# A hybrid layer's experts: rows gathered as the pair before is turned, indices one pair sooner, place 6's pages loaded in front of a test

## The chip, the cores and the metric

The kernel runs on one core of a Trainium2 chip. The metric is the device time of one execution in microseconds (us), as the median of several runs. TensorE (PE) multiplies, VectorE (DVE) and ScalarE (ACT) work element by element, GpSimd (POOL) issues the indirect DMAs and SyncE (SP) issues the loads of weights.

## What is computed

One layer: a mixer of retention, mLSTM and dilated attention, a layer norm, then a mixture of 32 experts over 512 tokens of width 1024, and a last layer norm. Each token goes to its top 4 experts. The change lies in the mixture; this is its reference, cut to what matters:

```python
logits = (xt @ w_router + b_router).astype(jnp.float32)      # 512 x 32
top_val, top_idx = lax.top_k(logits, TOP_K)                  # 4 of 32
probs = jax.nn.softmax(top_val, axis=-1)
...                                # rows of one expert stand in blocks of 128
def block(acc, inp):
    e, tok, p = inp
    xb = xt[tok]                                             # gathered rows
    gate = jnp.minimum(xb @ w_gate[e] + b_gate[e], SWIGLU_LIMIT)
    up = jnp.clip(xb @ w_up[e] + b_up[e], -SWIGLU_LIMIT, SWIGLU_LIMIT)
    y = ((up + 1.0) * gate * jax.nn.sigmoid(SWIGLU_ALPHA * gate)) @ w_down[e] + b_down[e]
    return acc.at[tok].add(y * p[:, None]), None
```

w_gate, w_up and w_down of an expert are 1024 x 1024 in float32, 4 MB each, so 384 MB of weights pass through the core.

## The kernel before

**Places and pages.** Experts are ranked by their number of tokens and put on 32 places (`ranks`, `placed`). Place 0 and the odd places take up to 96 rows, the other even places up to 64 (`small`, `size`). A place has 12 pages of weights, 128 x 2048 floats (1 MB) each: four each of gate, up and down, by halves of the output (`nh`) and of the input (`kh`). SP loads a page into one of ten raw buffers (`raws`, `fetch`, `load`, L85). ACT rounds it to float32r (`split_to`, L89) and DVE takes the rest (L90), and PE multiplies high and low parts (L117, L957). One page in twelve is used whole and not split (`unsplit`, L966). `chunk_of` splits up to two pages ahead of the one that PE wants.

**Pairs.** After places 0 and 1 the loop runs over pairs (e, e + 1), e = 2, 4, ..., 28. In the step of e stand, in this order of writing: gate and up of the pair (`gate_up_of`), every second step the indices of the next four places (`indices`, `IB` = 4), the gathers of the next pair (`gather_of`), and the down products of the pair before (`down_and_add`). Between the two halves of these, the next pair's rows are turned (`turned_x`: PE transposes to `txT`, L896 for 96 rows, L909 for 64, then ACT and DVE split them).

**Rows.** `indices` makes one-hot tiles on DVE (L636), multiplies them on PE (L1022) and finishes on DVE (L644 to L648, into `gi` and `wi`). `gather_of` is an indirect DMA of POOL (L940) from `x1d` in HBM into `xgs[e % 2]`: one buffer for the small places and one for the others, so a gather can start once the place two before is turned. `scatter` (L945) adds results from `ygs[e % 2]` to `yb` in HBM; each scatter waits until the one before has landed.

**The test.** At e = `FB` = 6 the order is another one: the down products of places 4 and 5 follow those of 2 and 3 at once, and then `further_blocks` tests a count (`novi`, L1060, L1069) and runs a loop over blocks that did not fit. With these inputs the count is zero. Every engine takes the test as a branch. In `chunk_of` pages of place 6 are not taken up before e is 6, and in the queues none of them is loaded or split in front of the test; on SP 28 register loads for later pages (L851) stand there. Place 7 is turned only behind the test, and 8 and 9 at the end of that step.

**Order.** A scheduler builds the queues of the engines from the order of writing, the dependences and its own estimates; on each engine instructions then run in the order of its queue, so one that waits holds up those behind it.

Of the kernel before, what the change touches and what calls it, by code (L numbers as in the profile page):

```python
# [20 lines left out]
E = 32  # L21
# [20 lines left out]
def hybrid_layer(ctx: ExitStack, tc: tile.TileContext, A, out):  # L42
# [11 lines left out]
    rp = [cst.tile([128, PAGE], F32R, tag=f"r{i}", name=f"r{i}") for i in range(NR)]  # L54
# [17 lines left out]
    raws = [fp[0], fp[1]]  # L72
# [29 lines left out]
    whi, wlo = [rp[4], rp[5]], [rp[6], rp[7]]  # L102
# [726 lines left out]
    FB = 6  # L829
# [29 lines left out]
    def flush():  # L859
        while later:  # L860
            later.pop(0)()

    def chunk_of(e):

        def f(n, nh, kh):
            last = seq[n, e, nh, kh] + len(whi) - 1
            while todo and seq[todo[0]] <= last and todo[0][:2] != ("w_down", L) and (todo[0][1] != FB or e >= FB):
                k = todo.pop(0)
                if k not in loaded:
                    fetch(1)  # L870
                w = loaded.pop(k)
                ready[k] = (w, None) if unsplit(k) else w if isinstance(w, tuple) else split_whole(w)
            with ExitStack() as es:
                for i in last_split:
                    es.enter_context(tc.issue_after(i))
                flush()
            return ready.pop((n, e, nh, kh))
        return f
# [12 lines left out]
    def transposed(src, name, page, m=C, whole=None):  # L891
        hl_ = page[:, 0:16 * m].rearrange("p (w a b) -> p w a b", w=2, a=8)
        for i in range(2):
            p = ps(f"t{name}_{i}")
            for k in range(4):
                PE.transpose(p[:, m * k:m * k + m], src[0:m, blk(4 * i + k)], ident[0:m, 0:m])  # L896
            s = slice(4 * i, 4 * i + 4)
            split_to(hl_[:, 0, s, :], hl_[:, 1, s, :], v3(p, 4, 4 * m))
            if whole is not None and i == 0:
                SC.activation(whole, v3(p, 4, 4 * m), AF.Copy)  # L900
        return hl_[:, 0], hl_[:, 1], whole
# [114 lines left out]
    def indices(e0, n):  # L1016
        p = ps(f"ix{e0}")
        for e in range(e0, e0 + n):
            j = 5 * (e - e0)
            o = one_hot(e, f"oh{e}")  # L1020
            for tb in range(NT):
                PE.matmul(p[0:C, j:j + 5], o[:, tb], RH[:, tb, e, :], start=tb == 0, stop=tb == NT - 1)  # L1022
        index_finish(p, n, C, gi[:, e0:e0 + n], wi[:, e0:e0 + n], f"ixf{e0}")
# [4 lines left out]
    def gate_up_of(*es, between=None):  # L1028
        parts = []
        for e in es:  # L1030
            if small(e):
                f = folds[e // 2 % 2]
                PO.tensor_copy(f[0:64, 0:CS], selr[0:64, e:e + 1].bitcast(F32).to_broadcast([64, CS]))
            parts.append((str(e), chunk_of(e), f if small(e) else selr[:, e:e + 1], xT.pop(e), hgs[e % 2], size(e), small(e)))
        return gate_up(parts, between)
# [22 lines left out]
    def further_blocks():  # L1058

        nov = nc.values_load(novi[0:1, 0:1], min_val=0, max_val=NB - 1)  # L1060
        jcol = cst.tile([NB, 4], F32, name="jcol")
        erow = cst.tile([1, NB], I32, name="erow")
        jrow = cst.tile([128, NB], F32, name="jrow")
        qe = cst.tile([128, NT, 1], F32, name="qe")
        je = cst.tile([128, 1], F32, name="je")
        re = cst.tile([128, NT, 1, 5], BF, name="re")
        gio = cst.tile([128, 1], I32, name="gio")
        wio = cst.tile([128, 1], F32, name="wio")
        with tc.If(nov > 0):  # L1069

            c0, c1, sml, c3 = (cnt[0:NB, i, :] for i in range(4))
            V.tensor_scalar(c0, c1, num[0:NB, 1:2], None, op0=OP.is_le)
            V.tensor_reduce(jcol[:, 0:1], c0, axis=AX.X, op=OP.add)
            V.tensor_tensor(c3, c1, c0, op=OP.mult)
            V.tensor_reduce(jcol[:, 1:2], c3, axis=AX.X, op=OP.max)
            V.tensor_scalar(jcol[:, 0:1], jcol[:, 0:1], float(E - 1), None, op0=OP.min)
            V.scalar_tensor_tensor(c3, iota_e[0:NB], jcol[:, 0:1], sml, op0=OP.is_equal, op1=OP.mult, accum_out=jcol[:, 3:4])
            V.tensor_scalar(jcol[:, 2:3], num[0:NB, 1:2], jcol[:, 1:2], 1.0, op0=OP.subtract, op1=OP.add)
            V.tensor_scalar(jcol[:, 2:3], jcol[:, 2:3], 128.0, float(C - 128), op0=OP.mult, op1=OP.add)
            V.tensor_tensor(jcol[:, 2:3], jcol[:, 2:3], jcol[:, 3:4], op=OP.subtract)  # L1080
            p = ps("ove")
            PE.transpose(p[0:1, 0:NB], jcol[:, 0:1], ident[0:NB, 0:NB])
            V.tensor_copy(erow, p[0:1, 0:NB])
            p = ps("ovj")
            PE.matmul(p[:, 0:NB], jcol[:, 2:3].to_broadcast([NB, 128]), ident[0:NB, 0:NB], start=True, stop=True)
            V.tensor_copy(jrow, p[:, 0:NB])
            main_raws = list(raws)
            raws[:] = raws[-1:]
            with tc.For_i(0, nov) as b:
                ev = nc.values_load(erow[0:1, ds(b, 1)], engines=(nc.sync.engine, nc.vector.engine), min_val=0, max_val=E - 1)  # L1090
                xv = nc.values_load(srt["of"][0:1, ds(ev, 1)], engines=(nc.sync.engine,), min_val=0, max_val=E - 1)
                V.tensor_copy(qe, qs[:, :, ds(ev, 1)])
                V.tensor_copy(je, jrow[:, ds(b, 1)])
                V.tensor_copy(re, RH[:, :, ds(ev, 1), :])
                V.tensor_copy(selr[:, E:E + 1], selr[:, ds(ev, 1)].bitcast(F32))
                p = ps("ovx")
                for tb in range(NT):
                    o = sm.tile([128, NT, C], BF, tag="ohs", name=f"ovo{tb}").rearrange("p t c -> p (t c)")[:, 0:128]
                    V.tensor_scalar(o, iota_s, je, qe[:, tb, :], op0=OP.add, op1=OP.is_equal)
                    PE.matmul(p[:, 0:5], o, re[:, tb, 0, :], start=tb == 0, stop=tb == NT - 1)  # L1100
                index_finish(p, 1, 128, gio, wio, "ixov")
                xo = v3(fp[11], 2)[:, 1, :]
                V.memset(xo, 0.0)
                gather(xo, gio)
                xTo = transposed(xo, "xTo", rp[0], 128)

                def chunk(n, nh, kh):
                    flush()
                    return split_whole(load(A[n][ds(xv, 1), nh, kh].rearrange("e p k f -> p (e k) f"), 4))

                gate_up([("o", chunk, selr[:, E:E + 1], xTo, hgs[0], 128, False)])
                flush()
                ho = transposed(hgs[0], "hTo", rp[1], 128)
                down([("o", chunk, ho, ygs[0], wio, 128, False)])
                flush()
                scatter(ygs[0], gio)
            cleared_folds()
            raws[:] = main_raws

    IB = 4  # L1120

# [18 lines left out]
    def turned_x(e):  # L1140
        if small(e):
            xT[e] = transposed_small(xgs[0], f"xT{e}", rp[2][:, 0:HALF])
        else:
            xT[e] = transposed(xgs[e % 2], f"xT{e}", rp[0], whole=xw)

    def gather_of(e):
        gather(xgs[e % 2][0:size(e)], gi[0:size(e), e:e + 1])
# [18 lines left out]
    PO.memset(xgs[0], 0.0)  # L1166
    turned_x(1)
    gate_up_of(1, between=first_indices)
    flush()
    for i, t in ((2, whi), (3, wlo)):  # L1170
        t.insert(0, cst.tile([128, PAGE], F32R, tag=f"f{i}", name=f"s{i}"))
# [16 lines left out]
    for e in range(2, L - 1, 2):  # L1188
        if e == FB:
            down_and_add(*before)  # L1190
            flush()
            further_blocks()
            turned_x(FB + 1)
        gate_up_of(e, e + 1)
        if e % IB == 2:
            indices(e + 2, IB if e + 2 + IB <= E else E - e - 2)
        for f in (e + 2, e + 3):
            if f < L:
                gather_of(f)
        if e == FB - 2:  # L1200
            count_blocks()
        def turned_next():
            for f in (e + 2, e + 3):
                if f < L and f != FB + 1:
                    turned_x(f)

        if e != FB:
            down_and_add(*before, between=turned_next)
        before = (e, e + 1)
        if e == FB:  # L1210
            flush()
        for f in before:
            turned_h(f)
        if e == FB:
            turned_next()
# [8 lines left out]
            PE.matmul(p, ident[0:1, 0:1].to_broadcast([1, 128]), ln2[0:1, i, c], start=True, stop=True)  # L1224
            SC.activation(ln2[:, i, c], p, AF.Copy)
    gate_up_of(L - 1)
    gather_of(L)
    PO.memset(rows, 0.0)
    down_and_add(*before)
    flush()  # L1230
    turned_h(L - 1)
    turned_x(L)
    down_and_add(L - 1)
    flush()
    zt = [v3(t, 2) for t in extra[1:3]]
# [168 lines left out]
```

## Time and profile before

| what | value |
|---|---|
| median of 3 runs | 1858.97 us |
| lowest and highest | 1857.85 and 1859.48 us |
| profiled execution, its own time | 1858.14 us |
| its span, first to last instruction | 1856.0 us |
| mean granted TensorE clock | 0.966 |
| PE, DVE and ACT busy | 92%, 69%, 58% of the span |

The span is 2.1 us shorter than the execution's own time. The first gather of an expert's rows starts at 642.7 us and the last scatter at 1808.1 us. Times in rows of a timeline are counted from the start of the span. The clock in a row of windows is the granted share of full speed: 1.00 is 2.4 GHz, 0.50 is 1.2 GHz.

### The profile page before, as it was taken

What the parts mean: (1) busy time and instruction counts of PE and PEld (TensorE: products, weight loads), DVE (VectorE), ACT (ScalarE), POOL (GpSimd) and SP (SyncE); (2) the same over time, 40 slices, a digit from 0 to 9 for tenths busy, and PEclk for the clock granted to TensorE, in tenths of its full rate; (3) what the DMA queues carried; (4) which work ended last, traced back from release to release, by engine and by line L of the source; (5) the groups of instructions that cost most, each with busy time, mean ns of one, the idle gap of its engine ahead of it and who ended that gap; (6) DMA issues with size and microseconds to landing.
All of it is one profiled execution on the core that took longest, in us unless ns stands there. A gap on an engine that the chain in (4) does not pass through costs nothing. (4 is left out here: it accounts for less than half of the span.)

```text
span 1856.0 us, 21811 instructions
## 1 busy us (share of the span) xinstructions
PE 1706.1 (92%) x7566; PEld 1245.6 (67%) x7566; DVE 1275.5 (69%) x1342; ACT 1078.1 (58%) x1097; POOL 234.4 (13%) x133
## 2 busy tenths in 40 slices
PE   8999999999999899797989799899989989979886
PEld 6889877778888666564656566566656656656553
DVE  3444255654354888786778698788878868878776
ACT  4464325532232457575667587587677767867781
POOL 0000000000000410201110220220220220130114
PEclk9999999999999989898889999999989989989898
DMA  5212212153243469897989999989989989988795
GB/s 207 90 52 108 87 60 93 56 188 127 95 162 137 169 241 342 308 405 261 360 302 364 377 327 405 382 315 405 384 292 411 374 306 409 375 325 355 252 330 223
DMA packets 73808, 485.24 MB, mean 261 GB/s; under 512 B 9914, under 2 KB 10170, under 8 KB 18782
## 3 DMA queue, kind: packets, MB, share of 16 engines
q1 hardware_dynamic: 65742, 460.58, 64.2%
q0 software_dynamic: 7952, 23.22, 4.9%
q8 instruction: 61, 1.00, 0.2%
q14 instruction: 53, 0.43, 0.1%
HBM read 471.30 MB, written 16.91 MB: 263 GB/s over the span
## 5 line engine op out<-in xcount | busy, mean ns | idle before, releaser
L90 DVE TENSOR_TENSOR r<-f,r 128x2048 fp32r<-128x2048 f32 (+3 forms) x249 | 450.8, 1818 | 281.8 <-ACT r L89 272.7
L89 ACT ACTIVATE r<-f 128x2048 fp32r<-128x2048 f32 (+3 forms) x249 | 380.0, 1536 | 192.5 <-PE pg L117 35.1
L117 PE MATMUL gu<-r,r 128*96 128x512 f32 x924 | 233.4, 398 | 3.0 <-DVE r L90 2.3
L117 PEld LDWEIGHTS gu<-r,r 128*96 128x96 f32 x924 | 148.8, 163 | 68.9 <-DVE r L90 5.2
L957 PE MATMUL gu<-r,xh 128*128 128x512 f32 x632 | 183.3, 422 | 4.0 <-DVE r L90 3.6
L90 DVE TENSOR_TENSOR s<-f,s 128x2048 fp32r<-128x2048 f32 x68 | 155.4, 2286 | 23.0 <-ACT s L89 18.8
L117 PE MATMUL dn<-r,h 128*96 128x512 f32 x516 | 144.6, 415 | 27.5 <-ACT r L89 22.5
L90 DVE TENSOR_TENSOR r<-g,r 128x2048 fp32r<-128x2048 f32 x68 | 154.9, 2287 | 19.3 <-ACT r L89 19.1
L957 PEld LDWEIGHTS gu<-r,xh 128*128 128x128 f32 x632 | 120.4, 192 | 50.0 <-issue 15.8
L945 POOL DMA_INDIRECT yb<-f,gi x31 | 80.9, 2609 | 533.6 <-ACT f L1012 432.1
L89 ACT ACTIVATE r<-g 128x2048 fp32r<-128x2048 f32 x68 | 129.8, 1918 | 26.3 <-PE gu L117 13.6
L117 PE MATMUL pg<-x,r 128*128 128x512 f32 x576 | 138.5, 399 | 0.0
L89 ACT ACTIVATE s<-f 128x2048 fp32r<-128x2048 f32 x68 | 129.8, 1909 | 13.2 <-PE gu L117 4.2
L117 PEld LDWEIGHTS dn<-r,h 128*96 128x96 f32 x516 | 82.2, 169 | 74.0 <-ACT r L89 28.5
L117 PEld LDWEIGHTS pg<-x,r 128*128 128x128 f32 x576 | 107.9, 188 | 25.4 <-issue 0.2
L940 POOL DMA_INDIRECT f<-x1d,gi x31 | 82.5, 2660 | 251.7 <-DVE wi L648 102.6
L957 PE MATMUL dn<-r,xh 128*128 128x512 f32 x328 | 96.8, 419 | 4.7 <-DVE r L90 4.0
L957 PE MATMUL gu<-s,xh 128*128 128x512 f32 x328 | 94.7, 419 | 5.1 <-DVE s L90 3.6
L117 PE MATMUL gu<-s,r 128*96 128x512 f32 x372 | 93.3, 395 | 0.5 <-DVE s L90 0.5
L89 ACT ACTIVATE xh<-txT 128x256 fp32r<-128x256 f32 x30 | 11.3, 383 | 120.7 <-PE txT L909 120.5
L957 PEld LDWEIGHTS gu<-s,xh 128*128 128x128 f32 x328 | 61.9, 191 | 28.7 <-DVE s L90 6.8
L90 DVE TENSOR_TENSOR s<-g,s 128x2048 fp32r<-128x2048 f32 x32 | 73.2, 2287 | 7.7 <-ACT s L89 7.6
(387 smaller groups left out, 2683.5 us busy)
## 6 DMA issues: line engine op xcount, KB each, us to landing
f<-in_w_gate_dram SPq DMA_DIRECT2D x80, 1024.0 KB, 6.4
f<-in_w_up_dram SPq DMA_DIRECT2D x79, 1024.0 KB, 7.5
f<-in_w_down_dram SPq DMA_DIRECT2D x77, 1024.0 KB, 11.5
g<-in_w_down_dram SPq DMA_DIRECT2D x39, 1024.0 KB, 12.5
g<-in_w_up_dram SPq DMA_DIRECT2D x34, 1024.0 KB, 9.7
g<-in_w_gate_dram SPq DMA_DIRECT2D x32, 1024.0 KB, 6.8
l<-in_w_gate_dram SPq DMA_DIRECT2D x16, 1024.0 KB, 7.2
l<-in_w_up_dram SPq DMA_DIRECT2D x15, 1024.0 KB, 8.7
```

The source lines that it names most:

```text
L89: a = SC.activation(hi, src, AF.Copy)
L90: last_split[:] = [a.ins, V.tensor_tensor(lo, src, hi.bitcast(F32), op=OP.subtract).ins]
L117: PE.matmul(po, l(k), r(k), start=first and n == 0, stop=last and n == 3 * len(ks) - 1)
L940: nc.gpsimd.indirect_dma_start(out=dst, out_offset=None, in_=src, in_offset=bass.IndirectOffsetOnAxis(ap=idx, axis=0), bounds_check=S - 1, ...
L945: nc.gpsimd.indirect_dma_start(out=yb, out_offset=bass.IndirectOffsetOnAxis(ap=idx, axis=0), in_=src, in_offset=None, bounds_check=S - 1, ...
L957: PE.matmul(p, xT[:, 4 * kh + k, :], w[:, k, :], start=kh + j + k == 0, stop=kh + j == 2 and k == 3, skip_group_check=True)
```

## The change

Six things are edited.

- In the prologue `indices(IB, 2)` is added behind the gate and up products of place 1, so places 4 and 5 have their indices there. In the loop `indices` now makes e + 4 to e + 7 in place of e + 2 to e + 5.
- The gathers of the next pair are written ahead of the step's gate and up products.
- All places from 4 on are turned in `turned_next`: place 7 no longer behind the test, place 31 no longer behind the loop.
- `chunk_of` no longer holds place 6's pages back, so they are split on while the down products of 4 and 5 run.
- `fetch(len(raws) - 2)` ahead of the test issues more loads of pages in front of it.
- The loop in the branch then uses only the first buffer of `raws`, `whi` and `wlo`, and another page for its turned rows. It has no turns with these inputs.

```diff
-            while todo and seq[todo[0]] <= last and todo[0][:2] != ("w_down", L) and (todo[0][1] != FB or e >= FB):
+            while todo and seq[todo[0]] <= last and todo[0][:2] != ("w_down", L):
...
-            main_raws = list(raws)
-            raws[:] = raws[-1:]
+            main = [list(t) for t in (raws, whi, wlo)]
+            for t in (raws, whi, wlo):
+                t[:] = t[:1]
...
     gate_up_of(1, between=first_indices)
+    indices(IB, 2)
     flush()
...
             down_and_add(*before)
             flush()
+            fetch(len(raws) - 2)
             further_blocks()
-            turned_x(FB + 1)
+
+        for f in (e + 2, e + 3):
+            gather_of(f)
         gate_up_of(e, e + 1)
-        if e % IB == 2:
-            indices(e + 2, IB if e + 2 + IB <= E else E - e - 2)
-        for f in (e + 2, e + 3):
-            if f < L:
-                gather_of(f)
+        if e % IB == 2 and e + 4 < E:
+            indices(e + 4, min(IB, E - e - 4))
...
             for f in (e + 2, e + 3):
-                if f < L and f != FB + 1:
-                    turned_x(f)
+                turned_x(f)
...
     gate_up_of(L - 1)
-    gather_of(L)
...
     turned_h(L - 1)
-    turned_x(L)
     down_and_add(L - 1)
```

**POOL in the steady part.** f_80 is the row buffer of the small places and f_76 that of the others as long as the row is L940; in the scatters (L945) f_80 and f_74 are result buffers. Before, from the scatters of places 10 and 11 on:

```order
L945 DMA yb<-f_80,gi 512x1024
L945 DMA yb<-f_74,gi 512x1024
L940 DMA f_80<-x1d,gi 64x1024
L940 DMA f_76<-x1d,gi 96x1024
L940 DMA f_80<-x1d,gi 64x1024
L1033 CAST h_4361<-selr 64x64
L940 DMA f_76<-x1d,gi 96x1024
```

The four gathers are those of 16, 17, 18 and 19: two pairs' gathers stand together. Now, from the scatters of places 8 and 9 on:

```order
L945 DMA yb<-f_80,gi 512x1024
L945 DMA yb<-f_74,gi 512x1024
L940 DMA f_80<-x1d,gi 64x1024
L1033 CAST h_4361<-selr 64x64
L940 DMA f_76<-x1d,gi 96x1024
L945 DMA yb<-f_80,gi 512x1024
L945 DMA yb<-f_74,gi 512x1024
```

Here the gathers are those of 16 and 17, and the last two rows the scatters of 10 and 11: the gathers moved in front of two scatters, and every pair now has the same pattern.

**PE at the turn of places 4 and 5**, between the two halves of place 1's down products (dn_0, dn_1). Before:

```order
L117 MATMUL dn_0_5046<-s_4512,h_4361 96x512 x4
L117 MATMUL dn_1_5114<-r_86,h_4361 96x512 x8
L117 MATMUL dn_1_5114<-r_88,h_4361 96x512 x4
L117 MATMUL dn_1_5114<-r_85,h_4361 96x512 x4
L909 MATMUL txT_0_5085<-ident,f_80 128x96 x4
L909 MATMUL txT_1_5092<-ident,f_80 128x96 x4
```

Now:

```order
L117 MATMUL dn_0_5064<-s_4530,h_4361 96x512 x4
L909 MATMUL txT_0_5103<-ident,f_80 128x96 x4
L909 MATMUL txT_1_5110<-ident,f_80 128x96 x4
L896 MATMUL txT_0_5117<-ident,f_76 128x96 x4
L896 MATMUL txT_1_5125<-ident,f_76 128x96 x4
L117 MATMUL dn_1_5132<-r_86,h_4361 96x512 x8
```

The transposes moved ahead of the second half.

**ACT in front of the test.** dn_0 and dn_1 are the halves of the down products of 4 and 5, `f_73` holds the last page of place 5. Before:

```order
L1012 ACTIVATE f_80<-dn_0_5838,wi 64x512
L1012 ACTIVATE f_74<-dn_0_5839,wi 96x512
L89 ACTIVATE r_85<-f_73 128x2048
L960 ACTIVATE bhl<-dn_1_5942 64x512
L1012 ACTIVATE f_80<-dn_1_5942,wi 64x512
L1012 ACTIVATE f_74<-dn_1_5943,wi 96x512
L1060 TENSOR_LOAD novi
```

Now:

```order
L1012 ACTIVATE f_80<-dn_0_5871,wi 64x512
L1012 ACTIVATE f_74<-dn_0_5872,wi 96x512
L89 ACTIVATE r_85<-f_73 128x2048
L89 ACTIVATE s_4529<-f_79 128x2048
L960 ACTIVATE bhl<-dn_1_5975 64x512
L1012 ACTIVATE f_74<-dn_1_5976,wi 96x512
L1012 ACTIVATE f_80<-dn_1_5975,wi 64x512
L89 ACTIVATE r_85<-f_70 128x2048
L1060 TENSOR_LOAD novi
```

Two pages of place 6 (f_79, f_70) are now split in front of the test; the first two rows and what they wait for are as they were.

## Rows read from the trace of the kernel before

**Rows 1.** The page: busy us of engines; granted clock in 40 slices.

```profile
PE 1706.1 (92%) x7566; PEld 1245.6 (67%) x7566; DVE 1275.5 (69%) x1342; ACT 1078.1 (58%) x1097; POOL 234.4 (13%) x133
...
PEclk9999999999999989898889999999989989989898
```

**Rows 2.** Waits of PE: line, what ended them, us in total, times, longest.

```profile
PE txT L909 <- DMA f<-x1d,gi: 45.7, 6, 8.9
PE dn L117 <- ACT r L89: 22.5, 14, 8.3
...
PE txT L909 <- issue: 5.7, 1, 5.7
...
PE txT L896 <- PEq L1069: 3.9, 1, 3.9
```

**Rows 3.** Timeline of PE, two neighbouring turns: start, us, work [idle before <-releaser].

```profile
1054.30 1.07 PE L957 MATMUL dn<-r,xh 128*128 128x512 f32 x4
1063.27 0.87 PE L909 MATMUL txT<-ident,f 96*128 96x96 f32 x4 [7.90 <-DMA f<-x1d,gi]
...
1130.05 0.49 PE L909 MATMUL txT<-ident,f 96*128 96x96 f32 x4
```

**Rows 4.** Timeline of POOL over the first of these turns.

```profile
1048.42 7.28 POOL L940 DMA_INDIRECT f<-x1d,gi  x1 [20.68 <-DVE wi L648]
...
1066.82 2.69 POOL L940 DMA_INDIRECT f<-x1d,gi  x1 [9.81 <-PE txT L909]
```

**Rows 5.** Windows from first down matmul to same later matmul (columns: busy, clock, DMA).

```profile
core 0: us, PE busy (x) PEld busy (x) DVE busy (x) ACT busy (x) POOL busy (x), PEclk, DMA share, GB/s
1054.30:1067.25 12.95, 5.05 (x20) 3.73 (x19) 1.81 (x3) 3.02 (x4) 2.83 (x3) 0.74 0.86 301
...
1629.93:1642.47 12.54, 5.61 (x21) 4.10 (x20) 2.38 (x3) 3.58 (x5) 3.41 (x3) 0.63 0.86 313
sum 63.72, PE 26.89 PEld 19.70 DVE 10.69 ACT 16.75 POOL 15.83; mean PE 5.38 PEld 3.94 DVE 2.14 ACT 3.35 POOL 3.17
...
1129.14:1133.59 4.45, 3.66 (x20) 2.56 (x19) 1.22 (x2) 2.96 (x4) 0.00 (x0) 1.00 1.01 418
```

**Rows 6.** Windows of gate and up products, of two pairs, and of two DMA extremes.

```profile
1012.04:1054.30 42.26, 40.75 (x174) 27.77 (x173) 37.38 (x28) 30.48 (x22) 11.24 (x3) 1.00 0.98 380
...
1089.74:1129.14 39.40, 39.40 (x158) 27.19 (x157) 35.72 (x20) 30.47 (x22) 5.32 (x2) 1.00 0.98 377
...
989.65:1133.59 143.94, 130.11 (x564) 89.67 (x563) 117.06 (x85) 104.45 (x91) 25.79 (x10) 0.98 0.94 358
...
1120.00:1144.00 24.00, 21.80 (x100) 15.22 (x99) 19.05 (x15) 16.06 (x16) 1.06 (x1) 1.00 1.01 420
...
840.00:858.00 18.00, 16.67 (x72) 10.76 (x71) 15.31 (x10) 16.10 (x15) 2.66 (x1) 1.00 0.33 105
```

**Rows 7.** Timeline of PE: turn of place 4, and around the test.

```profile
774.22 1.51 PE L909 MATMUL txT<-ident,f 96*128 96x96 f32 x8 [8.86 <-DMA f<-x1d,gi]
...
874.17 3.73 PE L117 MATMUL dn<-r,h 128*96 128x512 f32 x8 [8.31 <-ACT r L89]
...
883.41 1.51 PE L896 MATMUL txT<-ident,f 96*128 96x96 f32 x8 [3.87 <-PEq L1069]
...
887.83 2.07 PE L957 MATMUL gu<-s,xh 128*128 128x512 f32 x4 [1.19 <-ACT s L89]
...
942.26 1.51 PE L909 MATMUL txT<-ident,f 96*128 96x96 f32 x8 [5.69 <-issue]
```

**Rows 8.** Windows right behind two of these waits.

```profile
774.22:779.90 5.68, 5.51 (x23) 4.17 (x24) 3.15 (x4) 3.19 (x5) 1.45 (x2) 0.50 0.53 164
942.26:947.10 4.84, 4.84 (x21) 4.19 (x22) 1.87 (x5) 3.70 (x6) 1.92 (x2) 0.50 0.23 66
```

**Rows 9.** Timelines of ACT and of POOL around the test.

```profile
871.64 0.68 ACT L1012 ACTIVATE f<-dn,wi 96x512 f32<-96x512 f32 x1 [9.00 <-DMA yb<-f,gi]
...
890.91 3.72 POOL L1033 CAST h<-selr 64x64 fp32r<-64x64 f32 x2
```

More of the change, by code (lines that the diff above doesn't have):

```diff
@@ L1104, in further_blocks @@
                 gather(xo, gio)
-                xTo = transposed(xo, "xTo", rp[0], 128)
+                xTo = transposed(xo, "xTo", rp[1], 128)
                 def chunk(n, nh, kh):
@@ L1117, in further_blocks @@
             cleared_folds()
-            raws[:] = main_raws
+            for t, m in zip((raws, whi, wlo), main):
+                t[:] = m
     IB = 4
```

## The prediction

> **What bounds the kernel now.** I read the page first. PE is busy for 92% of the span, DVE for 69%, and the granted clock falls below full speed in single slices, most of them in the second half, where the experts run [rows 1]. So PE sets the time, and what can be won is its idle time and the time at the lower clock behind that. The waits of PE say what the idle time is made of: 45.7 us in six waits of L909, the transposes that turn a small place's rows, each ended by the landing of the gather; 8.3 us in one wait for a split on ACT; 5.7 us in one more turn; 3.9 us behind a branch [rows 2].
>
> The timeline of two neighbouring turns shows the pattern. In one, the transpose at 1063.27 starts 7.90 us late, behind a gather; in the next, at 1130.05, no wait stands [rows 3]. POOL explains it: the gather for the first turn starts at 1048.42, when DVE has just made the indices (releaser `wi`, L648), and its issue takes 7.28 us; the gather for the second turn starts at 1066.82, right behind the transposes that free its buffer, 63 us ahead of use [rows 4]. Indices come four places at a time and just ahead of the first of the two pairs, so every second pair waits.
>
> **What the change does, part by part.**
>
> *Steady part.* The queue of POOL now gives each pair the pattern that the second pair had, and the indices are there one pair sooner. What a wait costs is read from one stretch of the program, from the first down matmul of a pair to the same later matmul: 12.95 to 13.21 us and less with the wait, 63.72 us for all five, against 4.45 us in a pair without [rows 5]. Both hold the same matmuls; the difference also holds the time at 1.2 GHz behind the wait, where the clock column reads 0.62 to 0.74. So 63.72 - 5 x 4.45 = **41.5 us** go. What is late next there? Nothing that the row of the pair without wait does not hold already (its own small waits are in the 4.45). The index work stays: the gate and up stretch with it takes 42.26 us, the one without 39.40 [rows 6], 2.86 us for each call on four places, before and after.
>
> *The same wait at places 4 and 5.* There PE waits 8.86 us [rows 7], and then 5.68 us run at clock 0.50 with PE busy for 5.51 [rows 8]; at full clock that work takes half, so 8.86 + 2.84 = **11.7 us** go. The added `indices(IB, 2)` makes this possible. By the 2.86 us for four places it adds about 1.4 us in the prologue; the last call makes two places in place of four and gives 1.4 back. Net 0, with bounds of -1.4 and +1.4, as the prologue may hide it or not.
>
> *Places 8 and 9 behind the test.* The wait of 5.69 us at 942.26 [rows 7] stands behind the same late indices; the 4.84 us behind it run at 0.50 with PE busy throughout [rows 8]. 5.69 + 2.42 = **8.1 us** go, since place 9 is then gathered in front of the test and place 8 by POOL right behind it, 45 us ahead of use.
>
> *Test.* In front of it, PE waits 8.31 us at 874.17 for a split on ACT [rows 7]; ACT itself waits 9.00 us there for a scatter to land, before it may write the next result into the same buffer [rows 9]. That scatter, its buffer and ACT's order around it are as they were, so I keep this stall. Bounds: the scatters now share the DMA engines with pages of place 6, which SP issues in a stretch where the engines were busy for only 0.33 [rows 6], so it may grow by some 3 us; it may also end sooner, at most by its 8.3. The branch itself costs 3.87 us on PE [rows 7] and stays. Behind the branch, PE waits 1.19 us more for the first split of place 6 [rows 7]. Two pages are now split in front of the test, so this goes: **1.2 us**. The turn of place 7 and the bias matmuls between 883.41 and 887.83 are moved, not removed; bounds for this piece are 0 and 4.4 us. The pages in front of the test bring nothing more: what PE waited for there was ACT, not a page.
>
> *What else is moved.* On POOL, the gathers pass two scatters. Behind a gather stand the copy of the fold (L1033) and two scatters; in the pair without wait the same queue held the same pieces, and its cost is in the 4.45. Behind the test the folds of 6 and 8 now follow one gather, where they started at 890.91 [rows 9]; no row says how long PE can do without the first of them, so the gather's 2.69 us [rows 4] bound the cost at 0 and 2.7; I take 0, as the gate products of place 6 come before the fold. On SP 28 register loads go from the front of the test to places between later loads; PE does not wait for pages there. On ACT and DVE the splits of place 7's rows move ahead of the test, beside down products. Place 31's turn moves from the end into the last pair's down products, the same eight transposes. The loop in the branch has no turns: nothing.
>
> **Sum.** 41.5 + 11.7 + 8.1 + 1.2 = 62.5 us. From the profiled execution's own 1858.14 (span 1856.0 and 2.1 around it) that is 1795.6; the median lies 0.8 above that execution, so **1796 us**.
>
> **Rivals.**
>
> *The DMA engines become the bound.* Two pairs, one with and one without wait, take 143.94 us and move 358 GB/s, or 51.5 MB, at a busy share of 0.94 [rows 6]. Without 8.3 us of wait the same bytes need 380 GB/s, and a share of 0.94 x 143.94 / 135.6 = 1.0. If 358 were all that there is, the five pairs would keep their time as waits for pages, and only 11.7 + 8.1 + 1.2 would be won: 1838 us. For it speaks the share; against it the window of 24 us at 420 GB/s [rows 6], at which the 51.5 MB take 123 us, and that the waits of PE name no page among their largest [rows 2]. 12%. The Trainium skill bears on this: "DMA: Bandwidth & Descriptors", Where 436 GB/s comes from, says that for loads from HBM about 358 GB/s per core bind, not the fabric's 435. By that rule this rival would be the result, 1838 us. The 24 us at 420 do not agree with it.
>
> *The change doesn't do what it says:* the gathers stand earlier in the queue but still land late, because POOL reaches them no sooner, the indices being the last to come. Then only the piece behind the test is won, about 1857 us, no change. Against it: indices are made in the step before, some 66 us ahead, as for the second pair. 4%.
>
> *Slower: every pair waits.* Gathers now stand in front of two scatters and behind a fold's copy that waits for PE. If a pair's gather is issued only within 9 us of its turn, the six or seven pairs that have no wait today get one of 8.3 us (41.5 / 5), while the others keep theirs: 1858 + 6 x 8.3 = 1908 us. It decides from the point where POOL's queue holds a gather back for over 54 us of the 63 that it has; the gather at 1066.82 was held for nothing but its buffer [rows 4]. 4%.
>
> **How the numbers follow.** The forecast has 80%: 1796, with its own bounds. Downward: the stall in front of the test goes (8.3) and the rest of that piece comes (3.2): 1784. Upward: the scatters take 3 more, the fold 2.7, the prologue 1.4, and the index work, whose delay of 2.86 the old wait hid from what follows, shows in up to five pairs with up to 2.9 each: 1796 + 21.6 = 1818. The range is 1784 to 1818; it leaves out the rivals with 20%. A measurement of this kernel can tell about 0.2% (3.7 us) from no change. Faster by more: 80 + 12 = 92%; within: 4%; slower: 4%.
>
> **What would show it.** In the profile after, the row of PE L909 ended by the gather should be gone or below 1 us in all, the clock at 1.0 over the steady part, two pairs at about 135.6 us, and the page at 95% for PE. The gathers of POOL should start right behind the transposes of the pair before. The 8.3 us of L117 and 3.9 us of L1069 should still stand. I am wrong if ACT, DVE or PE have rows of waits for pages in the steady part and the DMA share reads 1.0 there (the first rival), or if L909 still waits for gathers (the others).

## The result, and the profile after

The changed kernel takes 1795.18 us (median; 1792.76 to 1797.79), the kernel before in the same comparison 1858.41 (1857.68 to 1859.48): a ratio of 0.966, 95% interval 0.9642 to 0.9678. The prediction was 1796, range 1784 to 1818. The profiled execution of after took 1792.76 us, with a span of 1790.9; the span of before was 1856.0, so 65.1 us are gone in the trace, where the sum said 62.5.

The page of after: busy us of the engines, and the granted clock in 40 slices.

```profile
PE 1690.2 (94%) x7566; PEld 1232.0 (69%) x7566; DVE 1275.7 (71%) x1346; ACT 1078.5 (60%) x1097; POOL 179.8 (10%) x133
...
PEclk9999999999999998999899999999999999999898
```

Against [rows 1] PE is busy for 94% (92% before), and of the dips of the clock in the second half only two at the end are left: full speed (2.4 GHz) from 878.7 to 1670.6 us. POOL is busy for 179.8 us in place of 234.4, in part because a gather of the steady part takes 1.0 us where one whose indices came last took 7.28 [rows 4].

The waits of PE in after, the largest and the new one (us in total, times, longest):

```profile
PE dn L117 <- ACT r L89: 24.5, 17, 9.8
...
PE gu L957 <- DVEq L1069: 5.4, 1, 5.4
```

The row of L909 behind the gather, 45.7 us in [rows 2], does not exist any more, nor does the 5.7. The stall in front of the test is there, 9.8 in place of 8.3. Behind the test PE now waits 5.4 us for DVE's sequencer, where [rows 2] has 3.9 for PE's own.

A turn of the steady part in after (timeline of PE):

```profile
1168.14 1.07 PE L957 MATMUL dn<-r,xh 128*128 128x512 f32 x4
1169.05 0.49 PE L909 MATMUL txT<-ident,f 96*128 96x96 f32 x4
```

And the queue of POOL ahead of it:

```profile
1101.99 1.00 POOL L940 DMA_INDIRECT f<-x1d,gi  x1 [26.93 <-PE txT L909]
1103.80 1.06 POOL L1033 CAST h<-selr 64x64 fp32r<-64x64 f32 x1 [0.82 <-PE gu L974]
1107.89 1.01 POOL L940 DMA_INDIRECT f<-x1d,gi  x1 [3.02 <-PE txT L896]
```

The transposes at 1169.05 start at once. Their rows were gathered at 1101.99, 67 us earlier, and that gather waited for nothing but the transposes that free its buffer, as the prediction wanted it. Two windows of after: two pairs, and the stretch from the gate products of places 4 and 5 to the down products of 6 and 7 (us, busy of PE, PEld, DVE, ACT, POOL, granted clock, DMA share, GB/s):

```profile
1234.58:1370.32 135.74, 129.06 (x565) 88.53 (x564) 117.15 (x84) 104.55 (x90) 16.74 (x10) 1.00 1.00 386
...
773.72:963.08 189.36, 169.29 (x725) 117.87 (x724) 151.48 (x111) 131.82 (x108) 20.64 (x13) 0.96 0.93 361
```

The second stretch in before:

```profile
783.18:985.03 201.85, 176.63 (x727) 120.94 (x725) 150.87 (x112) 131.81 (x109) 24.84 (x13) 0.92 0.86 329
```

Two pairs take 135.74 us (143.94 in [rows 6], forecast 135.6). The stretch around the test is 12.5 us shorter, where 8.1 + 1.2 were forecast.

Two questions are left. Which part of the change earns this, and why did the stretch around the test give 12.5 us where its terms said 9.3? And the DMA share reads 1.00 now: is the forecast's first rival there after all, a little further on?

### The profile page after: what moved, and what is told of

Read it like the earlier page. It is cut to its first block, busy times and chain, and to the rows that moved or that the text cites. A ratio compares the mean times of both kernels' runs of the same rounds, so it can differ in the third digit from the quotient of the medians.

```text
span 1790.9 us, 21812 instructions
## 1 busy us (share of the span) xinstructions
PE 1690.2 (94%) x7566; PEld 1232.0 (69%) x7566; DVE 1275.7 (71%) x1346; ACT 1078.5 (60%) x1097; POOL 179.8 (10%) x133
## 5 line engine op out<-in xcount | busy, mean ns | idle before, releaser
L117 PE MATMUL dn<-r,h 128*96 128x512 f32 x516 | 140.3, 406 | 28.4 <-ACT r L89 24.5
L945 POOL DMA_INDIRECT yb<-f,gi x31 | 72.7, 2345 | 437.4 <-ACT f L1012 342.9
L940 POOL DMA_INDIRECT f<-x1d,gi x31 | 44.1, 1423 | 450.0 <-PE txT L909 366.8
L117 PEld LDWEIGHTS gu<-s,r 128*96 128x96 f32 x372 | 59.9, 161 | 26.1 <-DVE s L90 1.0
## 6 DMA issues: line engine op xcount, KB each, us to landing
g<-in_w_down_dram SPq DMA_DIRECT2D x39, 1024.0 KB, 12.5
```

The source lines that it names most:

```text
L117: PE.matmul(po, l(k), r(k), start=first and n == 0, stop=last and n == 3 * len(ks) - 1)
L940: nc.gpsimd.indirect_dma_start(out=dst, out_offset=None, in_=src, in_offset=bass.IndirectOffsetOnAxis(ap=idx, axis=0), bounds_check=S - 1, ...
L945: nc.gpsimd.indirect_dma_start(out=yb, out_offset=bass.IndirectOffsetOnAxis(ap=idx, axis=0), in_=src, in_offset=None, bounds_check=S - 1, ...
```

## Experiments

### Which part: the indices, the place of the gathers, or the pages

**Indices alone** (before, with two edits; gathers stay behind the gate and up products, place 6's pages as in before):

```diff
     gate_up_of(1, between=first_indices)
+    indices(IB, 2)
...
-        if e % IB == 2:
-            indices(e + 2, IB if e + 2 + IB <= E else E - e - 2)
+        if e % IB == 2 and e + 4 < E:
+            indices(e + 4, min(IB, E - e - 4))
```

> The kernel before, with the indices computed one pair sooner and nothing else: the gathers are still written behind the gate and up products, the turn of place 7 still stands behind the test. Theory (what the turns waited for was the indices, and any gather that has them early enough lands some 50 us before its turn, wherever it is written): 1795 to 1800 us, no wait of TensorE for a gather of over 1 us in the steady part. Rival (the place of the gathers is half of it, since GpSimd takes them up behind the casts and the scatters): a wait of 3 us or more stays in each turn, 1810 us or above.

Measured: 1795.28 us, ratio 0.9662 (0.9641 to 0.9682). Two pairs:

```profile
1169.00:1304.73 135.73, 128.99 (x565) 88.53 (x564) 117.11 (x85) 104.57 (x90) 17.02 (x10) 1.00 1.00 387
```

That is the whole gain. Where the gathers are written is worth nothing that can be measured, once their indices are early: two pairs take 135.73 us here and 135.74 in after.

**Pages alone** (before, with the guard, the fetch and the lists of buffers as in after):

```diff
-... todo[0][:2] != ("w_down", L) and (todo[0][1] != FB or e >= FB):
+... todo[0][:2] != ("w_down", L):
...
+            fetch(len(raws) - 2)
             further_blocks()
```

> The kernel before, with the part on place 6's pages alone: they are fetched and the first split in front of the test; gathers and indices as before. Theory: the 1.19 us wait for the first split goes, the wait behind the test grows by about 1.5: 1858 us, between 1855 and 1860, and all stalls of 11 to 13 us in the turns stand. Rival (this part has a gain of its own of 5 us or more): 1853 or less.

Measured: 1856.97 us, ratio 1.0005 (0.9991 to 1.0019). No gain that stands out of the interval of 2.6 us to either side, and all stalls stand. PE's waits there:

```profile
PE txT L909 <- DMA f<-x1d,gi: 45.5, 6, 9.1
PE dn L117 <- ACT r L89: 23.0, 14, 9.9
...
PE txT L896 <- DVEq L1069: 5.3, 1, 5.3
```

The stall in front of the test is 9.9 and the one behind it 5.3, as in after: both are longer with this part of the change.

**All but the pages** (after, with the guard back and the fetch gone; the loop in the branch keeps the lists of buffers of after):

> The kernel after, with the part on place 6's pages undone: neither are the pages fetched nor is one of them split in front of the test; gathers and indices as after. Theory (the time lies in the turns alone, the test's part is worth about nothing): 1795 us, between 1792 and 1799; in the trace the 5.4 us that TensorE waits behind the test goes back to about 3.9, and a wait of about 1.2 for the first split of place 6 comes back behind it. Rival (the pages in front of the test are what took the wait away, 5 us or more): 1800 or above, with a wait on a page of place 6 of 5 us or more.

Measured: 1797.41 us, ratio 0.9691 (0.9668 to 0.9715), which overlaps the interval of after. The timeline of PE around the test:

```profile
855.80 2.73 PE L117 MATMUL dn<-r,h 128*96 128x512 f32 x8 [3.74 <-ACT r L89]
...
861.43 1.17 PE L963 MATMUL gu<-bhl,selr 128*96 128x512 f32 x4 [0.82 <-ACTq L1069]
869.98 2.07 PE L957 MATMUL gu<-s,xh 128*128 128x512 f32 x4 [7.37 <-ACT s L89]
```

ACT behind the test:

```profile
868.01 1.91 ACT L89 ACTIVATE s<-f 128x2048 fp32r<-128x2048 f32 x1 [6.68 <-DMA f<-in_w_gate_dram]
```

The time is as the theory has it; the waits are neither's. The stall in front is 3.74 in place of 9.81, the one behind the test 0.82 in place of 5.38, and then 7.37 come for a page of place 6, which SP asks for only behind the test. The rival's wait of over 5 us is there, and it has a price: the stretch from the gate products of places 4 and 5 to the down products of 6 and 7, 189.36 us in after, takes 7.3 us longer here,

```profile
770.19:966.87 196.68, 175.52 (x724) 119.45 (x723) 151.53 (x111) 132.02 (x108) 20.55 (x13) 0.95 0.88 341
```

but only 1.1 longer in indices alone, where SP loads no page of place 6 in front of its test either:

```profile
773.47:963.96 190.49, 172.97 (x724) 118.67 (x723) 151.60 (x111) 131.47 (x108) 22.14 (x13) 0.96 0.93 359
```

In the profiled execution 3.5 of the 7.3 us are made up for ahead of place 4, in the prologue. The queue of SP tells the two kernels apart. SP is past its own test early in both, at 841.7 and 844.5 us, but its first load behind it starts here at

```profile
861.41 0.34 SPq L85 DMA_DIRECT2D f<-in_w_gate_dram  x1
```

and in indices alone at

```profile
845.86 0.34 SPq L85 DMA_DIRECT2D f<-in_w_gate_dram  x1
```

Here SP waits in between for the tests of DVE and ACT:

```profile
SPq L85 <- DVEq L1069: 15.2, 1, 15.2
SPq L85 <- ACTq L1069: 3.2, 1, 3.2
```

By the code, the first load goes into the buffer that the loop in the branch uses in after, where before uses the last one. So this run does not undo the whole part on the pages: the lists stayed, and with them the fetch in front of the test is needed. Changing the lists alone was not tried.

### What PE waits for behind the test

**Fetch, but no split in front** (after, with the guard back):

> The kernel after, where the pages of place 6 are still fetched in front of the test, but none is split there. Theory (the wait behind the test grew from 3.87 to 5.38 us because VectorE comes to the test late, behind the split that now stands in front): VectorE reaches the test some 2 us sooner, TensorE's wait behind the test is 3.5 to 4.2, and the kernel takes 1793 to 1795 us, 0 to 1.5 less than after. Rival (the wait is the branch's own, whatever VectorE does): 5.4 stays, and the first split comes on top of it: 1796 to 1798.

Measured: 1794.93 us, ratio 0.9665 (0.9649 to 0.9681). The edit did not do what was meant. With the pages landed, the order that is recorded for ACT and DVE still puts two splits, of a page of place 6 and one of place 7, in front of the test, and now both behind the last results of places 4 and 5. The timeline of DVE:

```profile
869.19 4.49 DVE L90 TENSOR_TENSOR r<-f,r 128x2048 fp32r<-128x2048 f32 x2 [5.82 <-ACT r L89]
874.01 1.06 DVE L636 TENSOR_TENSOR oh<-iota_s,qs 128x384 bf16<-128x384 bf16 x2 [0.33 <-DVEq L1069]
```

And of PE:

```profile
873.88 0.71 PE L963 MATMUL gu<-bhl,selr 128*96 128x512 f32 x1 [7.25 <-DVEq L1069]
```

It answers the question all the same, as a dose. With no split between the last results and the test, PE waits 0.82 us behind it (pages left out) or 0.30 (indices alone); with one, 5.38 in after; with two, 7.25. In after that split stands in these rows, on ACT, then on DVE, which waits for ACT; DVE's test comes behind it, and then PE starts:

```profile
871.01 1.90 ACT L89 ACTIVATE r<-f 128x2048 fp32r<-128x2048 f32 x1
...
872.94 2.29 DVE L90 TENSOR_TENSOR r<-f,r 128x2048 fp32r<-128x2048 f32 x1 [3.07 <-ACTq L1069]
...
875.43 3.60 PE L957 MATMUL gu<-s,xh 128*128 128x512 f32 x8 [5.38 <-DVEq L1069]
...
L1069 PEldq COMPARE_BRANCH  x1: 368/368/368, 868.4 to 868.4; - x1
```

So the 5.38 are DVE's lateness: PE's own branch, the last row, was long over. By the order of writing in the kernel the page is one of place 7; the section on the change takes both pages split there for place 6's. Place 6's second page goes into the split buffers that the loop in the branch uses, and ACT splits it only behind the test. The forecast's 3.87 were something else: PE's own branch instruction, which the listing of line 1069 shows (ns min/median/max, and when), in before:

```profile
L1069 PEldq COMPARE_BRANCH  x1: 6007/6007/6007, 877.1 to 877.1; - x1
```

in pages alone:

```profile
L1069 PEldq COMPARE_BRANCH  x1: 6010/6010/6010, 876.9 to 876.9; - x1
```

and in indices alone:

```profile
L1069 PEldq COMPARE_BRANCH  x1: 367/367/367, 865.5 to 865.5; - x1
```

It took 6.0 us in before and in pages alone (there DVE's lateness comes on top: its last event stands at 883.8, 0.9 us behind the end of PE's branch), and 0.37 to 0.47 in every kernel here with the earlier indices, also in indices alone, whose code around the test is written as in before. What makes it long was not tried; it stays open.

### What holds the stall in front of the test

**A third result buffer** (after, with place 5's results in `rows`, free until the last place, and the further blocks' numbers copied out of that tile):

```diff
+    result_of = lambda e: rows if e == FB - 1 else ygs[e % 2]
...
-hT.pop(e), ygs[e % 2], wi[...]
+hT.pop(e), result_of(e), wi[...]
...
-scatter(ygs[e % 2][0:size(e)], ...)
+scatter(result_of(e)[0:size(e)], ...)
```

> The kernel after, with one result buffer more: place 5's rows go to the tile `rows`, which is free until the last place, so that ScalarE need not wait for the scatter of place 3 before it copies place 5's first half out (for this the expert numbers that the further blocks read are copied out of that tile, one small instruction on VectorE). Nothing is left out. Theory (the 8.3 us in front of the test, 9.8 after, hang on that one buffer): TensorE's wait of 9.8 us in front of the test goes to under 1.5, the half clock behind it (10.2 us, worth about 5) goes with it in part, the wait behind the test stays at 5 to 6: 1781 to 1787 us. Rival (the wait is handed on: the scatters stand in a chain of some 10 us each, and what is late next is as late): 1792 to 1796, with a wait of 5 us or more at another place between 850 and 880 us.

Measured: 1789.18 us, ratio 0.9637 (0.9606 to 0.9669). PE's waits:

```profile
PE dn L117 <- ACT r L89: 15.4, 17, 1.2
...
PE gu L957 <- DVEq L1073: 5.4, 1, 5.4
PE gu L974 <- POOL h L1033: 4.5, 1, 4.5
```

The queue of POOL:

```profile
869.56 3.13 POOL L945 DMA_INDIRECT yb<-f,gi  x1 [3.56 <-DMA yb<-f,gi]
876.99 0.95 POOL L1234 MEMSET f<- 96x1024 f32 x1 [4.30 <-DMA yb<-f,gi]
...
881.09 0.42 POOL L1033 CAST h<-selr 64x64 fp32r<-64x64 f32 x2
```

The 9.8 go entirely, so they hung on that one buffer, as the theory has it. But the time is 2 us above its range: 4.5 us come back as a wait for the fold copy of place 6, which stands on POOL behind two scatters, a memset of the very tile that became the buffer, and a gather. The prediction took that copy at 0, with a bound of 2.7. In after, PE comes to it so late that it costs nothing; when the stall goes, its cover goes.

**Fold copy earlier** (the same, with the copy written in front of the down products of 4 and 5):

> e5_third_result, with the fold copy of place 6 on GpSimd written in front of the down product of places 4 and 5 (and once more behind the further blocks, inside the test), so that it no longer stands behind their scatters. Theory (the 4.5 us that TensorE waits for that copy in e5 is GpSimd's place in its queue): the wait of 4.5 goes, the wait behind the test stays at 5.4, 1783 to 1787 us. Rival (another thing is as late there): a wait of 3 us or more stays within 15 us behind the test, 1788 to 1790.

Measured: 1784.97 us, ratio 0.961 (0.9594 to 0.9627). The wait of 4.5 is gone, the 5.4 stay.

**And no split in front of the test** (the same, with a loop over the further blocks that uses two pairs of split buffers, so that no split can be drawn ahead of it):

> e8_third_fold, where the loop over the further blocks uses two of the three pairs of split buffers in place of one; with that no split of a page of place 7 can be drawn in front of the test, where in after one stands between the last results and the test on ScalarE and VectorE. Theory (the wait behind the test is VectorE's lateness: none of 0.3 to 0.8 us with no split there in e1 and e3, 5.4 with one, 7.3 with two): TensorE's wait behind the test is under 1.2 us, a new wait of 1 to 3 us for the first splits comes behind it, 1779 to 1785 us. Rival (the branch itself costs TensorE about 4 to 6, as in before): the wait stays at 3.9 or more, 1784 to 1788.

Measured: 1786.26 us, ratio 0.9625 (0.9605 to 0.9644): no gain over the kernel ahead. Its timeline of PE:

```profile
858.18 2.09 PE L957 MATMUL gu<-s,xh 128*128 128x512 f32 x8 [0.96 <-DVEq L1077]
...
875.64 0.80 PE L974 MATMUL gu<-bhl,h 128*128 128x512 f32 x1 [7.06 <-POOLq L1077]
```

And of POOL:

```profile
874.59 0.95 POOL L1240 MEMSET f<- 96x1024 f32 x1 [3.91 <-DMA yb<-f,gi]
```

The wait behind the test fell to 0.96, as the theory wanted. What it did not see: POOL comes to the test only at 875 us, behind the scatter of place 5 and that memset, and the first fold product waits for POOL to be past it. In the kernel ahead the same product starts at 876.26, just after, and so hides it.

**Indices, third buffer, fold copy** (before, with these three alone):

> e3_indices_alone (the kernel before with the indices one pair sooner) with the two edits of e8 on top: place 5's results in a third buffer, place 6's fold copy written earlier. The change's part on place 6's pages is not in it, nor are the gathers written sooner. Theory (that part is worth nothing, also once the wait in front of the test is gone): e3's wait of 7.1 us in front of the test goes, the 2.3 us for the first split of place 6 stay or grow by 1 to 2, 1782 to 1787 us, as e8 within 3. Rival (without the pages split in front, the splits of place 6 become the wait that takes the place of the removed one): a wait of 6 us or more behind the test, 1789 or above.

Measured: 1784.29 us, ratio 0.9615 (0.959 to 0.9639). PE around the test:

```profile
855.28 0.85 PE L896 MATMUL txT<-ident,f 96*128 96x96 f32 x8 [0.30 <-PEq L1077]
...
859.35 1.49 PE L957 MATMUL gu<-s,xh 128*128 128x512 f32 x4 [2.30 <-ACT s L89]
```

As the theory has it, to the 2.3: the part on the pages is worth nothing here either. This and the kernel with fold copy and pages are the fastest here; the intervals of both lie below that of after.

### How far the transfers are from being the bound

**Useless loads.** Behind every fourth page of places 8 to 27 a quarter of it is loaded again into an unused tile:

```diff
                 loaded[k] = load(w, 4)
+                if 8 <= k[1] < 28:
+                    extra_pages[0] += 1
+                    if extra_pages[0] % 4 == 0:
+                        nc.sync.dma_start(v3(f6, 1, 512), w[:, 0:1, :])
```

The rates in the two expectations that follow count the pages alone (371 GB/s for after); the windows count gathers and scatters too (386).

> The kernel after, with useless transfers: behind every fourth page of places 8 to 27 its first quarter (262 KB) is loaded once more, into a part of a tile that nobody reads any more; 60 such loads, 15.7 MB. Two pairs then load 53.5 MB in place of 50.3 MB, 394 GB/s at 135.75 us. Theory (the stall was latency of the gather, and the page transfers still have room): within 5 us of after, 1795 to 1800, two pairs 135.8 to 136.7 us. Rival (with the stalls gone the transfers are the bound, at the 371 GB/s that the steady part of after shows): 15.7 MB at 371 GB/s is 42 us more: 1837, two pairs 144 us.

> The same with a quarter behind every second page: 120 loads, 31.5 MB more; two pairs load 56.6 MB, which is 417 GB/s at 135.75 us. Theory (the wall stands where the stretch of before with the highest rate stood, 420 GB/s): 1795 to 1815, two pairs 136 to 140 us. Rival (bound at 371 GB/s): 85 us more, 1880, two pairs 152.6 us.

Measured: 1815.74 us (ratio 0.9784, 0.9745 to 0.9823) and 1856.68 us (1.0009, 0.9987 to 1.003). Neither theory nor rival: by the medians 15.7 MB cost 20.6 us (23 by the ratios to before), the next 15.7 MB 40.9, which is 384 GB/s. SP had waits in both for the quarter before to land, so the first was made again with two places in turn:

> e4_quarter_in_4 with the useless quarters going to two places in turn, so that SyncE need not wait at each of them for the one before to land. Theory (the transfers have their wall at about 392 GB/s, gathers and scatters included, where after moves 387; SyncE's waits in e4 cost nothing): two pairs 139 to 143 us, 1812 to 1820. Rival (SyncE's waits in e4 made the loss, the transfers still have room): two pairs under 137 us, 1795 to 1802.

Measured: 1814.87 us, ratio 0.977 (0.9746 to 0.9793), the same, as the theory has it: SP's waits did not make the loss. Windows of two pairs, here:

```profile
1174.79:1313.28 138.49, 129.58 (x565) 88.54 (x565) 117.32 (x85) 104.78 (x91) 16.55 (x11) 1.00 1.02 398
1313.28:1455.28 142.00, 130.52 (x565) 88.34 (x565) 117.67 (x85) 104.95 (x91) 16.46 (x11) 1.00 1.01 395
```

and with a quarter behind every second page:

```profile
1108.09:1262.70 154.61, 134.70 (x566) 87.33 (x565) 118.13 (x85) 105.89 (x91) 18.00 (x11) 1.00 1.00 382
```

The transfers have a wall: with these loads two pairs move 382 to 398 GB/s with either dose; after moves 386. **An eighth left out** asks from the other side:

```diff
+                if 8 <= k[1] < 28 and k[2:] == (1, 1) and k[0] != "w_gate" and k[1] % 4 < 3:
+                    loaded[k] = v3(next_page(), 4)
+                else:
+                    loaded[k] = load(w, 4)
```

> The kernel after without the loads of 30 of the 240 pages of places 8 to 27 (six of the 48 of two pairs); what stands in the buffers is split and multiplied in their place, so that the results are other numbers. Theory (TensorE sets the pace of after, 129.0 of 135.75 us busy, the rest waits of about 1 us for splits): two pairs 135.4 to 135.8 us, 1793 to 1797, while the DMA share falls to about 0.9. Rival (at a DMA share of 1.00 the transfers set the pace): two pairs 133 us or less, 1785 or less.

Measured: 1786.11 us, ratio 0.9615 (0.9593 to 0.9637).

```profile
1167.31:1300.95 133.64, 127.36 (x567) 88.89 (x566) 116.76 (x85) 104.31 (x90) 17.53 (x10) 1.00 0.92 346
```

Between the two again, nearer to the rival: two pairs lose 2.1 us. Of these, 0.4 are PE's idle time (135.74 - 129.06 = 6.7 against 6.3) and 1.7 its busy time, for the same matmuls (565 and 567 of them on record). So in after PE waits for no page, but an eighth of the page loads costs it about 1.5%, and the 6% more bytes of quarters apart cost 2 to 5% more (138.5 and 142.0 for 135.74). Why the matmuls get shorter with fewer transfers was not separated from small waits that the busy time may hold.

## Why the prediction was right

**Steady part, 41.5 us: right in mechanism and size.** From the starts of the gate products, the five pairs lose 8.42, 7.67, 9.15, 8.25 and 8.25 us, 41.7 in all. Indices alone shows that it was the indices, as [rows 4] had been read; the gathers could have stayed where they were. The last call of `indices`, which makes two places in place of four, gave another 1.2.

**Places 4 and 5, 11.7: right.** The shift grows by 12.0 us between the gate products of places 2 and 4.

**Prologue, 0 with bounds of 1.4: not to be told from one execution.** The down product of place 0 starts 2.5 us later in after, 1.0 earlier in "all but the pages", which has the same call. The stretch at half clock around 680 us lasted 13.7 us in before, 17.1 in after, 10.2 there; that is more than the term. The 2.5 us lie outside the bounds. With them the pieces add up to -2.5 + 12.0 + 12.5 + 41.7 + 1.2 = 64.9 of the 65.1 us.

**Around the test, 8.1 + 1.2: mis-sized, and near in sum only by luck.** It gave 12.5, of which indices alone has 11.4. The wait of 5.69 us behind late indices went, as forecast. Four other terms were off. That the branch costs PE 3.87 us "and stays" did not hold: with early indices that branch takes 0.37 us, and DVE's lateness of 5.38 took its place. The prediction priced that at nothing: it counted two pages "now split in front of the test" as a gain of 1.2 and did not ask what their splits hold up on ACT and DVE. "I keep this stall" held in kind, not in size (9.81 for 8.31, within its bounds). "The loop in the branch has no turns: nothing" left out the loop's buffers, for which, by the code, SP waits 18.4 us in all but the pages; in after the loads issued in front of the test cover that. And the clock: I gave back half of 4.84 us behind one wait. In the whole stretch PE's busy time fell by 7.3 us and its idle time by 5.2, as the mean granted clock rose from 0.92 to 0.96. The next time, such a term is to be read as in the steady part, from a whole stretch with and without the wait, not wait by wait.

**Pages in front of the test, 1.2: no gain shown.** Pages alone shows 1.0005; 1.2 us lie within its interval.

**The first rival** had 12% at 358 GB/s. The wall is real, and at most some 3% above what after moves. The Trainium skill, "DMA: Bandwidth & Descriptors", Where 436 GB/s comes from, puts it at about 358 for loads from HBM; the 395 and 398 of the run with quarters apart do not agree. My sign for it had two halves, a DMA share of 1.0 and rows of waits for pages. After shows the first, at 1.00, and not the second: from 900 to 1660 us no wait of PE, ACT or DVE names a page. The share alone would have misled. Had a pair held 6% more bytes, this rival would have taken a third of the gain, as the useless loads did (20.6 of 63), and the 420 GB/s of 24 us in [rows 6], by which I set it aside, would have misled me: no stretch of two pairs kept that rate.

**The other two rivals** are out: the gathers do land early, and no pair waits.

## What to carry to other kernels

When every second step of a loop waits for a transfer, look at what the transfer's issue waited for; here the small computation of its addresses was late, and moving that alone by one step gave all of the 3.4%. Where several engines meet at a test, price what is drawn in front of it on each: one page's split, 1.9 us on ACT and then 2.3 on DVE, made PE's wait 4.6 us longer, and in three kernels here a wait that went came back from another engine (DVE in after, POOL in two of the others). A loop that is never entered can have a price too, where it shares buffers with the work behind it; here that was read from the code and the waits, and not tried alone. Before counting on more, add a dose of useless transfers: it showed that the next wall is at most some 3% away.

## What the runs showed of the hardware

The same branch, with a count of zero in every run, cost PE's sequencer 6.0 us in two kernels and 0.37 to 0.47 in the others, while ACT, DVE and POOL took 0.05 to 0.08 in all. The Trainium skill, "Runtime: NRT & Kernel Launch", Instruction fetch mechanics, warns that a taken branch may have to fetch its target's instructions; no run here shows whether that happened, or what was fetched.

PE's busy time for the same 565 matmuls of two pairs, all at 2.4 GHz, was longer with more transfers: 127.4 us at 346 GB/s, 129.1 at 386, 130.5 at 395 and 129.6 at 398, and 134.7 at 382 in the run with a quarter behind every second page. Small waits may be part of it.
